# A down projection by seven block products in both halves of the sequence, its weight sums made under the convolution and its gate applied at the end

## The chip, the cores and the metric

The kernel is one decoder layer on one core of a Trainium2 chip. The metric is the device time of one execution in microseconds. Before the change it is 2389.77 us, the median of three runs (2389.1 to 2391.83).

## The reference

Sequence length 2048, model width 1024, eight attention heads of 64, a short gated convolution beside the attention, and a feed-forward part of width 2816. Cut to what the change touches:

```
h2 = rmsnorm(x, norm2_g) * (1 + sc2) + sh2
u = causal_dwconv(h2 @ w_up, ffn_conv_w)        # (2048, 5632), three taps
u_gate, u_val = jnp.split(u, 2, axis=-1)
y = (jax.nn.silu(u_gate) * u_val) @ w_down      # (2048, 2816) @ (2816, 1024)
return x + g2 * y
```

All arrays are float32. The gate g2 belongs to the output column, so it may be multiplied into the columns of w_down or applied to the product.

## The kernel before, in words

The layer runs in stages on one core: the modulation and the first norm, the projections of v, k and q, the short convolution (`for j in range(4)`, `for ch in range(4)`, three products of 24 matmuls each), the attention, the output projection with the second norm, and then up and down, each in two halves of 1024 tokens: `up(0)`, `down_plain`, `up(1)`, `down_seven`.

**Up** goes over 22 pairs of column blocks (128 columns of the gate, 128 of the value). Each pair takes seven block products of 12 float16 matmuls instead of eight, in three PSUM banks X, Y and Z; banks come from ps_d (four banks) for even pairs and from ps_u (three) for odd ones. An eighth bank, ps_n, takes norm2's transposes. In the first half `up_weights` splits the next pair's weights into high and low float16 parts on ScalarE and VectorE, and `keep_weights` stores them; the second half loads them again. After the products come three taps of the convolution (L1495, L1500), silu, and the product y of gate and value (L1513 in the first half, L1517 in the second). `finish` of a pair runs in three steps inside the next pair.

**Down in the first half** (`down_plain`, L1587) stores y to `y_sc` and afterwards goes over four column and row blocks n and 22 steps i. A step loads 512 columns of y and of w_down side by side into one raw tile of 1024 columns (`load_pair`, L1379 to L1385), splits it into a high and a low part (`split_pair`: ScalarE at L1389, VectorE at L1390), and runs four tiles of three matmuls (high by high, high by low, low by high; they are recorded at L146, where `mm3` issues them). Splits run two steps ahead and loads five; the raw tiles and the tiles tagged "hi" and "lo" have four buffers each. The step before a block's last is left out and done together with the last. At the end of a block `add_gated` multiplies each of the four results by the gate and adds x1 (L1204, L1205), then stores it.

Beside this runs a side chain: the last pair's `finish`, then `norm2` for the second half's rows (loads of x1 at L1241, squares on ScalarE at L1245, transposes at L1228, some eleven VectorE operations for each of four column blocks), then the first loads for `up(1)`. One step of it follows steps 0, 1, 2 and then every second one.

**Down in the second half** (`down_seven`, L1623) works with seven products of 11 steps each, 77 for 88. With y and w_down cut into two by two blocks, it needs sums of blocks of y (t1 to t4, made by `down_inputs` in three steps behind each pair of `up(1)` and stored to `y_op`) and of w_down (s1 to s4, made by `down_weights` inside `up(1)` from columns already multiplied by the gate, and stored to `w_op`). The order of the products is in `plan`. The results are collected in two sets of four banks, ps_d for one and ps_u with ps_n for the other; x1 is added in advance on GpSimd (`gadd`, L1640).

**Order.** `K` pins the order of instructions on each engine to that of the program; nearly everything in these stages is pinned, SP's queue of DMA issues too. Stores of the sums are put off: `store_later` notes them and `flush` issues them (L1425) at the start of the next pair, at the start of `down_seven`, and at its fifth step.

Of the kernel before, what the change touches and what calls it, by code (L numbers as in the profile page):

```python
# [46 lines left out]
def kernel(  # L47
# [40 lines left out]
    y_sc = [dram.tile([P, S // 2], F32, name=f"y_sc{i}") for i in range(NPAIR)]  # L88
    y_op = {n: [dram.tile([P, 512], F32, name=f"y_{n}_{j}") for j in range(NJ)] for n in ("b11", "b21", "b22", "t1", "t2", "t3", "t4")}
    w_op = {n: [dram.tile([P, D], F32, name=f"w_{n}_{j}") for j in range(NJ)] for n in ("a11s3", "a12a22", "s1s2", "s4")}  # L90
# [62 lines left out]
    with ExitStack() as ph:  # L153
# [587 lines left out]

        def up_scales():
# [53 lines left out]
        for j in range(4):  # L796
# [5 lines left out]
            for ch in range(4):  # L802
# [7 lines left out]
                for name in ("x", "c", "b"):  # L810
# [379 lines left out]
    with ExitStack() as ph:  # L1190
# [188 lines left out]
        def load_pair(n, i):  # L1379

            Q, hf = divmod(n, 2)
            raw = raw_tile()
            K(nc.sync.dma_start(raw[:, 0:512], y_sc[i][:, Q * 512 : (Q + 1) * 512]))
            K(nc.sync.dma_start(raw[:, 512:1024], w_down[i * P : (i + 1) * P, hf * 512 : (hf + 1) * 512]))
            return raw  # L1385

        def split_pair(raw):
# [6 lines left out]
        plan = (("a11", "b11"), ("s2", "t2"), ("a12", "b21"), ("s3", "t3"), ("s1", "t1"), ("a22", "t4"), ("s4", "b22"))  # L1394
        place = {
            "a11": ("a11s3", 0), "s3": ("a11s3", 1), "a12": ("a12a22", 0), "a22": ("a12a22", 1), "s1": ("s1s2", 0), "s2": ("s1s2", 1),
            "s4": ("s4", 0),
        }

        def load_operands(p, j):  # L1400

            w, y = plan[p]
            n, e = place[w]
            raw = raw_tile()
            K(nc.sync.dma_start(raw[:, 0:512], y_op[y][j]))
            K(nc.sync.dma_start(raw[:, 512:1024], w_op[n][j][:, e * 512 : (e + 1) * 512]))
            return raw
# [3 lines left out]
        def first_pairs(load, hv):  # L1411

            for i in range(3):
                raws[0, i] = load(0, i)
# [16 lines left out]
        def down_inputs(i, y):  # L1431

            j = i // 2
            a, b = y[:, 0:512], y[:, 512:1024]
            if i % 2 == 0:
                t12 = fq.tile([P, 1024], F32, tag="lo", name="t12", bufs=4)
                K(nc.sync.dma_start(y_op["b11"][j], a))
                sub(t12[:, 0:512], b, a)
                store_later(y_op["t1"][j], t12[:, 0:512])
# [4 lines left out]
            K(nc.sync.dma_start(y_op["b21"][j], a))  # L1444
            K(nc.sync.dma_start(y_op["b22"][j], b))
# [3 lines left out]
            store_later(y_op["t2"][j], t12[:, 512:1024])  # L1449
            store_later(y_op["t3"][j], t34[:, 0:512])  # L1450
            store_later(y_op["t4"][j], t34[:, 512:1024])

        def down_weights(j):

            wa, wb = [fp.tile([P, 1024], F32, tag="first", name="wd", bufs=2) for _ in range(2)]
            for e, w in enumerate((wa, wb)):
                K(nc.sync.dma_start(w, w_down[(2 * j + e) * P : (2 * j + e + 1) * P, :]))
            yield
            wc, wd = [fq.tile([P, 1024], F32, tag="lo", name="wd", bufs=4) for _ in range(2)]
            a11, a21, a12, a22 = wa[:, 0:512], wa[:, 512:1024], wb[:, 0:512], wb[:, 512:1024]  # L1460
            s1, s2, s4 = wc[:, 0:512], wc[:, 512:1024], wd[:, 0:512]
            for w in (wa, wb):
                K(V.tensor_tensor(w, w, gates[:, D : 2 * D], op=ALU.mult))
                yield
            add(s1, a21, a22)
            sub(a21, a11, a21)
            yield
            sub(s2, s1, a11)
            sub(s4, a12, s2)
            for n, w in (("a11s3", wa), ("a12a22", wb), ("s1s2", wc)):  # L1470
                store_later(w_op[n][j], w)
            store_later(w_op["s4"][j][:, 0:512], s4)
            while True:
                yield

        def up(hv):
# [25 lines left out]
            def finish(i, p1, Y, gate, val, yg):  # L1502
# [19 lines left out]
            last = wsum = None  # L1522
            for i in range(NPAIR):
# [13 lines left out]
                else:  # L1537
                    wts = first_pairs(load_operands if hv else load_pair, hv)
                ops = next(wts)
                if hv and i % 2:  # L1540
                    next(wsum)
# [17 lines left out]
                if hv == 0:  # L1559
                    keep_weights(i)  # L1560
                elif i % 2:
                    next(wsum)
                else:
                    wsum = down_weights(i // 2)
                    next(wsum)
# [21 lines left out]
        def down_plain(side):  # L1587
# [32 lines left out]
            for _ in side:  # L1620
                pass
# [123 lines left out]
```

## Time and profile before

| what | us |
|---|---|
| median of three runs | 2389.77 |
| lowest, highest | 2389.1, 2391.83 |
| the profiled execution | 2394.71 |
| its span, first to last instruction | 2393.0 |
| TensorE busy | 2304.5 (96%) |
| VectorE busy | 1723.5 (72%) |
| ScalarE busy | 1172.7 (49%) |
| GpSimd busy | 358.6 (15%) |
| HBM traffic over the span | 178 GB/s |

In the profile PE is TensorE's matmul, PEld its weight load, DVE VectorE, ACT ScalarE, POOL GpSimd and SP the engine that issues most DMAs; a q behind the name is the engine's instruction queue. L1390 is line 1390 of the kernel. A row of the groups gives the engine, the operation, what is written and read with its shape, how many there are, their busy time in all and the mean of one in nanoseconds, then the idle time of the engine just before them and what ended most of it. A row of the chain gives start, duration and what the chain passed through. A row of the timeline gives start, duration, engine and line; the bracket at its end is the idle time of the engine before it and what released it. Times are microseconds from the first instruction. The busy time of matmuls that overlap is counted once, so their mean duration is longer than their pace.

### The profile page before, as it was taken

Reading aid. Unit: us, or ns where it says so; the run is one execution under the profiler, and the core shown is the slowest. Engines: PE = TensorE matmul, PEld = TensorE weight load, DVE = VectorE, ACT = ScalarE, POOL = GpSimd, SP = SyncE. Lnnn points to the kernel's source line nnn. Section 1 sums busy time; section 2 is a strip of 40 time slices with the busy share of each in tenths; the row PEclk is TensorE's granted clock in tenths of the full one; section 3 lists DMA queues with packets and bytes.
Section 4 is the critical chain, followed back from the end, with each engine's and each line's share of the span. In section 5 each row is a group of like instructions: output and inputs, shape, how many; then the busy total and the mean of one; then the engine's idle time right before and its main releaser. Section 6 shows DMA issues by size and latency. Waiting matters only on the chain.

```text
span 2393.0 us, 38865 instructions
## 1 busy us (share of the span) xinstructions
PE 2304.5 (96%) x14340; PEld 1385.3 (58%) x14340; DVE 1723.5 (72%) x3345; ACT 1172.7 (49%) x1997; POOL 358.6 (15%) x294
## 2 busy tenths in 40 slices
PE   5899999999899898999999999999999999998999
PEld 5765554444677676444444444688864444446887
DVE  6768885553999887466888888757747777676554
ACT  5745454320788896343655655555522222224332
POOL 0211111011677783001000000000000000000021
PEclk9999999999999999999999999999999999999999
DMA  9446596522899997434555554777666676675765
GB/s 264 148 147 186 158 263 187 155 83 84 164 183 190 196 191 166 137 119 158 181 180 199 193 181 169 261 232 239 219 217 224 212 268 214 217 266 188 245 228 194
DMA packets 447895, 461.03 MB, mean 193 GB/s; under 512 B 190720, under 2 KB 300632, under 8 KB 446680
## 3 DMA queue, kind: packets, MB, share of 16 engines
q1 hardware_dynamic: 440584, 441.70, 61.5%
q10 hardware_dynamic: 4752, 8.46, 1.0%
q0 software_dynamic: 2368, 8.39, 1.0%
q8 instruction: 112, 1.84, 0.3%
q14 instruction: 79, 0.65, 0.1%
HBM read 290.60 MB, written 134.28 MB: 178 GB/s over the span
## 4 chain that ended last, share of the span: by engine, by line
PE 86%; DVE 6%; ACT 3%; DMA 2%; issue 2%; SPq 1%; POOL 0%; DVEq 0%; ACTq 0%; POOLq 0%
PE acc L1487 33%; PE acc L146 22%; PE pr L146 10%; PE acc L1699 8%; PE pv L146 3%; PE pt L1068 2%; PE ps L1007 1%; PE ps L1008 1%; DVE near L1075 1%; PE po L1104 1%; DMA far<-wide 1%; DVE s_t L1031 1%; PE po L1106 1%; PE po L1105 1%; ACT s_t L1048 1%
## 5 line engine op out<-in xcount | busy, mean ns | idle before, releaser
L1487 PEld LDWEIGHTS <-pair 128*128 128x128 f16 x3696 | 361.6, 98 | 436.1 <-issue 0.3
L1487 PE MATMUL acc<-t,pair 128*128 128x512 f16 x2112 | 477.4, 379 | 0.0
L1487 PE MATMUL acc<-b,pair 128*128 128x512 f16 x1584 | 363.4, 379 | 0.0
L1390 DVE TENSOR_TENSOR lo<-raw,hi 128x1024 fp32r<-128x1024 f32 x165 | 201.9, 1244 | 138.2 <-ACT hi L1389 135.6
L1500 DVE SCALAR_TENSOR_TENSOR w<-w,fcw,w 128x1024 f32<-128x1024 f32 x176 | 226.1, 1285 | 54.3 <-ACT w L1495 48.1
L1389 ACT ACTIVATE hi<-raw 128x1024 fp32r<-128x1024 f32 x165 | 170.4, 1054 | 166.4 <-PE acc L1699 96.2
L1495 ACT ACTIVATE w<-w,fcw 128x1024 f32<-128x1024 f32 x88 | 100.7, 1144 | 189.1 <-DVE w L1293 189.1
L146 PEld LDWEIGHTS <-h 128*128 128x128 f16 x1344 | 130.2, 98 | 97.5 <-DVE h L359 5.3
L1640 POOL TENSOR_TENSOR u<-u,xs 128x512 f32<-128x512 f32 x4 | 6.0, 1531 | 1175.2 <-DMA raw<-w_s1s 1175.2
L146 PE MATMUL acc<-wp,mp 128*128 128x512 f16 x768 | 169.4, 379 | 1.1 <-DVE raw L960 1.0
L1048 ACT ACTIVATE s_t<-s_t,nb,cst 128x2048 f32<-128x2048 f32 (+15 forms) x128 | 164.7, 1288 | 4.8
L146 PE MATMUL acc<-hi 128*128 128x512 f32 x352 | 139.6, 397 | 1.6 <-DVE t L1204 1.6
L146 PE MATMUL acc<-lo,hi 128*128 128x512 f32 x352 | 137.3, 390 | 0.5 <-DVE lo L1390 0.5
L1060 POOL TENSOR_TENSOR wide<-s_t,wide 128x1024 f16<-128x1024 f32 x64 | 136.6, 2135 | 5.3
L146 PE MATMUL acc<-hi,lo 128*128 128x512 f32 x352 | 137.2, 390 | 0.0
L1031 DVE CUSTOM_DVE_ANT_0 s_t<-ps,nf,mx 128x512 f32<-128x512 f32 (+1 forms) x192 | 119.5, 643 | 17.7 <-PE ps L1010 9.4
L1699 PE MATMUL acc<-hi 128*128 128x512 f32 x308 | 121.4, 394 | 5.7 <-ACT hi L1389 5.7
L146 PE MATMUL pr<-h,wh 128*128 128x512 f16 x576 | 126.5, 379 | 0.0
L146 PE MATMUL pr<-h,wl 128*128 128x512 f16 x576 | 125.8, 379 | 0.0
L146 PEld LDWEIGHTS <-mp 128*128 128x128 f16 x768 | 74.9, 98 | 87.6 <-issue 1.3
L1699 PE MATMUL acc<-lo,hi 128*128 128x512 f32 x308 | 121.1, 393 | 0.9 <-DVE lo L1390 0.9
L1699 PE MATMUL acc<-hi,lo 128*128 128x512 f32 x308 | 120.8, 392 | 0.0
(361 smaller groups left out, 4552.3 us busy)
## 6 DMA issues: line engine op xcount, KB each, us to landing
up_sc<-pair SPq DMA_DIRECT2D x132, 256.0 KB, 3.0
pair<-up_sc SPq DMA_DIRECT2D x132, 256.0 KB, 4.8
wx<-in_w_up_dram SPq DMA_DIRECT2D x88, 256.0 KB, 3.3
raw<-in_w_up_dram SPq DMA_DIRECT2D x44, 512.0 KB, 3.8
raw<-y_sc SPq DMA_DIRECT2D x88, 256.0 KB, 3.2
raw<-in_w_down_dram SPq DMA_DIRECT2D x88, 256.0 KB, 4.2
wm<-in_w_ada_dram SPq DMA_DIRECT2D x128, 128.0 KB, 3.3
y_sc<-w SPq DMA_DIRECT2D x22, 512.0 KB, 2.7
```

The source lines that it names most:

```text
L146: ins = T.matmul(acc, lhsT=a, rhs=b, start=st, stop=sp)
L1007: K(T.matmul(ps[:, 0:cw], lhsT=qt, rhs=kh[:, c0 : c0 + cw], start=True, stop=False))
L1031: K(V.tensor_tensor_reduce(out=s_t[:, o0 + c0 : o0 + c0 + cw], in0=ps[:, 0:cw], in1=nf[:, c0 : c0 + cw], scale=1.0, scalar=-3.0e38 if g == ...
L1048: K(A.activation(cols, cols, AF.Exp, bias=nb[:, p : p + 1], scale=qk[:, 4:5], accum_out=un["l"][:, p : p + 1]))
L1060: K(G.tensor_tensor(wide[:, 1, :], s_t[:, WB * P : WU], wide[:, 0, :], op=ALU.subtract))
L1068: K(T.transpose(pt[:, b * P : (b + 1) * P], s_t[:, (b0 + b) * P : (b0 + b + 1) * P], ident))
L1389: K(A.activation(hi, raw, AF.Copy))
L1390: K(V.tensor_tensor(lo, raw, hi.bitcast(F32), op=ALU.subtract))
L1487: K(T.matmul(acc, lhsT=a, rhs=b, start=st, stop=sp, skip_group_check=True))
L1495: K(A.activation(y, u[:, 0:1024], AF.Copy, scale=fcw[:, ct : ct + 1]))
L1500: K(V.scalar_tensor_tensor(y, u[:, m : m + 1024], fcw[:, m * 44 + ct : m * 44 + ct + 1], y, op0=ALU.mult, op1=ALU.add))
L1699: K(T.matmul(acc[t], lhsT=a[:, c], rhs=b, start=st, stop=sp, skip_group_check=True))
```

## The change

Both halves of down now run the seven products, by one function `down(hv, side)` in place of `down_plain` and `down_seven`.

- The sums of w_down's blocks no longer carry the gate. A new generator `down_sums` makes them once, in the convolution stage, one step behind each product for the first three values of j: two loads of 512 KB and one store of 1 MB for each of 11 pairs of row blocks, and four additions or subtractions on VectorE. `down_weights`, its multiplications by the gate and its stores inside `up(1)` are gone. Blocks that are no sums are read from w_down itself.
- `down_inputs` runs behind each pair of both halves; y is no longer stored as a whole in the first half.
- The gate is applied by `finish_block` when a block is complete, with VectorE multiplying into a temporary and adding it to x1. GpSimd's additions are gone.
- The products stand in another order, in which a product that adds to the block before it follows it in the same banks; four new banks are taken at products 0, 2, 3 and 5, seven different ones in all, and ps_n is left to norm2.
- The side chain advances after steps 0, 1, 2, after even steps, and after steps with e % 7 == 1.

```diff
+        def down_sums():
...
+            for j in range(NJ):
+                if j + 1 < NJ:
+                    load(j + 1)
+                (a11, a21), (a12, a22) = [[w[:, 0:512], w[:, 512:1024]] for w in todo.pop(0)]
+                t = lp.tile([P, 2 * D], F32, tag="ws", name="ws", bufs=1)
+                s1, s2, s3, s4 = [t[:, n * 512 : (n + 1) * 512] for n in range(4)]
+                V.tensor_tensor(s1, a21, a22, op=ALU.add)
+                yield
+                V.tensor_tensor(s3, a11, a21, op=ALU.subtract)
+                V.tensor_tensor(s2, s1, a11, op=ALU.subtract)
+                yield
+                V.tensor_tensor(s4, a12, s2, op=ALU.subtract)
+                nc.sync.dma_start(w_sc[j], t)
+                yield
...
                     if j < 3:
                         next(convs[j + 1][2])
+                    next(wsums)
...
-        plan = (("a11", "b11"), ("s2", "t2"), ("a12", "b21"), ("s3", "t3"), ("s1", "t1"), ("a22", "t4"), ("s4", "b22"))
+        plan = (("a11", "b11"), ("a12", "b21"), ("s2", "t2"), ("s3", "t3"), ("a22", "t4"), ("s1", "t1"), ("s4", "b22"))
...
-                if hv == 0:
-                    K(V.tensor_tensor(yv, yg, yv, op=ALU.mult))
-                    nc.sync.dma_start(y_sc[i], yv)
-                else:
-                    y = fq.tile([P, 1024], F32, tag="hi", name="y", bufs=4)
-                    K(V.tensor_tensor(y, yg, yv, op=ALU.mult))
-                    down_inputs(i, y)
+                y = fq.tile([P, 1024], F32, tag="hi", name="y", bufs=4)
+                K(V.tensor_tensor(y, yg, yv, op=ALU.mult))
+                down_inputs(i, hv, y)
                 yield
...
+            def finish_block(c, n, t, total):
+                g = temp()
+                K(V.tensor_tensor(g, total, gate[n], op=ALU.mult))
+                add(xs[c, n][t], xs[c, n][t], g)
+                K(nc.sync.dma_start(out[rows[c][t], n * 512 : (n + 1) * 512], xs[c, n][t]))
 
             def evict(p, t):
                 a = acc[t]
                 if p == 0:
                     K(A.activation(u2[t], a, AF.Copy))
                 elif p == 1:
+                    finish_block(0, 0, t, a)
+                elif p == 2:
                     add(u2[t], u2[t], a)
...
                 elif p == 3:
                     add(u3[t], u2[t], a)
...
+                elif p == 5:
                     add(u3[t], u3[t], a)
+                    finish_block(1, 1, t, u3[t])
                 else:
+                    g = temp()
+                    add(g, u2[t], a)
+                    finish_block(*((0, 1) if p == 4 else (1, 0)), t, g)
+
+            extra = {(1, 2): (0, 0), (4, 2): (0, 1), (5, 2): (1, 1), (6, 3): (1, 0)}
...
-                if (p, j) == (0, 4):
+                if (p, j) in ((0, 0), (0, 4)):
                     flush()
...
+                if j == 0 and p in (0, 2, 3, 5):
+                    acc = banks({0: "dddd", 2: "uuud", 3: "dddu", 5: "uudd"}[p])
...
-                if e < 3 or e % 2 == 0:
+                if e < 3 or e % 2 == 0 or e % 7 == 1:
                     next(side, None)
...
-        down_plain(chain(up(0), steps[2], steps[3], kept_first()))
-        down_seven(up(1))
+        down(0, chain(up(0), steps[2], steps[3], kept_first()))
+        down(1, up(1))
```

More of the change, by code (lines that the diff above doesn't have):

```diff
@@ L740, in magnitudes, with load @@
                 seen[0] += 1
+        def down_sums():
+            todo = []
+            def load(j):
+                ab = [lp.tile([P, D], F32, tag="wd", name="wd", bufs=4) for _ in range(2)]
+                for e, w in enumerate(ab):
+                    nc.sync.dma_start(w, w_down[(2 * j + e) * P : (2 * j + e + 1) * P, :])
+                todo.append(ab)
+            load(0)
+            yield
[12 more added lines that the diff above has]
+                nc.sync.dma_start(w_sc[j], t)
+                yield
+            while True:
+                yield
+        wsums = down_sums()
         def up_scales():
@@ L1377, in first_weights @@
                 yield
[L1379 to L1385, printed above, removed]
         def split_pair(raw):
@@ L1429, in flush, with down_inputs @@
                 stores.pop(0)()
-        def down_inputs(i, y):
+        def down_inputs(i, hv, y):
             j = i // 2
+            cols = slice(hv * 512, (hv + 1) * 512)
             a, b = y[:, 0:512], y[:, 512:1024]
@@ L1448, in down_inputs @@
             sub(t34[:, 512:1024], a, t12[:, 512:1024])
[L1449 to L1474, printed above, removed]
+            store_later(y_op["t2"][j][:, cols], t12[:, 512:1024])
+            store_later(y_op["t3"][j][:, cols], t34[:, 0:512])
+            store_later(y_op["t4"][j][:, cols], t34[:, 512:1024])
         def up(hv):
@@ L1537, in up @@
                 else:
-                    wts = first_pairs(load_operands if hv else load_pair, hv)
+                    wts = first_pairs(hv)
                 ops = next(wts)
-                if hv and i % 2:
-                    next(wsum)
                 p1 = temp()
@@ L1623, in down_seven, with down @@
-        def down_seven(side):
+        def down(hv, side):
             todo = [(p, j) for p in range(7) for j in range(NJ)]
             loaded = split = 3
-            rows = [[slice((Q * 4 + t) * P, (Q * 4 + t + 1) * P) for t in range(4)] for Q in (2, 3)]
+            rows = [[slice((Q * 4 + t) * P, (Q * 4 + t + 1) * P) for t in range(4)] for Q in (2 * hv, 2 * hv + 1)]
             u2, u3 = [[fb.tile([P, 512], F32, tag=f"src{4 * n + t}", name="u") for t in range(4)] for n in range(2)]
+            gate = [gates[:, D + n * 512 : D + (n + 1) * 512] for n in range(2)]
@@ L1634, in x1_tiles, with banks @@
                     K(nc.sync.dma_start(xp, x1_sc[r.start // P][:, n * 512 : (n + 1) * 512]))
-            def write(c, n, t, src):
-                K(nc.sync.dma_start(out[rows[c][t], n * 512 : (n + 1) * 512], src))
-            def gadd(o, a, b):
-                K(G.tensor_tensor(o, a, b, op=ALU.add))
+            def banks(kinds):
+                return [
+                    ps_d.tile([P, 512], F32, tag="d", name="acc") if k == "d" else ps_u.tile([P, 512], F32, tag="u", name="acc")
+                    for k in kinds
+                ]
+            def finish_block(c, n, t, total):
[3 more added lines that the diff above has]
+                K(nc.sync.dma_start(out[rows[c][t], n * 512 : (n + 1) * 512], xs[c, n][t]))
             def evict(p, t):
```

109 lines of the change are left out of this document (21 added, 88 removed).

## The prediction

> **What bounds the kernel now.** I read the stretches by stage first, then the chain that ended last, then the waits inside single stages. Five stretches matter: the convolution group stage that gets the new weight sums, the two windows of up in the first half, down in the first half (plain), and down in the second half (seven products). The columns are microseconds, then each engine's busy time and instructions, the granted clock, the DMA share and GB/s.
>
> ```profile
> 340.00:598.00 258.00, 258.00 (x1221) 121.29 (x1220) 132.58 (x289) 71.96 (x161) 35.10 (x38) 1.00 0.45 137
> 1112.00:1316.00 204.00, 204.00 (x947) 92.47 (x946) 171.99 (x194) 114.28 (x169) 2.16 (x4) 1.00 0.49 172
> 1316.00:1519.00 203.00, 203.00 (x942) 92.27 (x941) 177.94 (x197) 118.71 (x176) 0.00 (x0) 1.00 0.54 189
> 1519.00:1771.00 252.00, 249.92 (x1125) 203.79 (x1124) 168.75 (x208) 123.72 (x148) 0.00 (x0) 1.00 0.70 233
> 2169.00:2393.00 224.00, 213.26 (x925) 174.94 (x923) 120.36 (x112) 82.98 (x81) 20.38 (x12) 0.97 0.67 225
> ```
>
> TensorE is the bound in all of them; it is idle only in down. But VectorE is busy for 178 of 203 us in up of the first half, and there the change adds work. The chain (start, length, what) and the groups give the pace of a down matmul and the counts:
>
> ```profile
> 1119.96 398.86 PE acc L1487 x1848
> 1518.82 40.84 PE acc L146 x180
> 1770.26 398.88 PE acc L1487 x1848
> 2169.13 5.48 PE acc L1699 x24
> 2174.63 0.70 DVE wd L1294
> 2175.35 0.75 SPq L1425
> 2177.38 4.44 DMA raw<-w_a11s
> 2183.02 1.24 DVE lo L1390
> 2204.57 184.37 PE acc L1699 x812
> 2389.03 0.69 DVE xs L1293
> L146 PE MATMUL acc<-hi 128*128 128x512 f32 x352 | 139.6, 397 | 1.6 <-DVE t L1204 1.6
> L1699 PE MATMUL acc<-hi 128*128 128x512 f32 x308 | 121.4, 394 | 5.7 <-ACT hi L1389 5.7
> ```
>
> 812 matmuls in 184.37 us is 0.227 us each, so a step (four tiles by three matmuls) takes 2.72 us. Each group is one of three alike: plain has 3 x 352 = 1056 matmuls, seven products have 3 x 308 = 924. Up takes 398.9 us for 22 pairs, 18.1 each. Plain runs from 1518.82 to 1770.26, 251.4 us against 1056 x 0.227 = 239.8; of the other 11.6, 2.1 is visible idle (252.00 less 249.92) and 9.5 goes with norm2's transposes. Seven runs from 2169.13 to 2388.94, 219.8 us against 209.8: all 10.0 lost lies before 2204.57.
>
> **The change, part by part.** The sum is made against the profiled execution, 2394.7 us (span 2393.0), 4.9 above the median of 2389.8; I carry its difference over to the median.
>
> *Matmuls of the first half:* 132 fewer, 132 x 0.227 = -30.0 us, all on the path.
>
> *Start of down in the second half.* What cost the 10.0 us is this row:
>
> ```profile
> 2171.91 0.69 DVE L1293 TENSOR_TENSOR wd<-wd 128x512 f32<-128x512 f32 x1 [5.62 <-PE acc L1699]
> ```
>
> The sums of the last w_down pair need a "lo" buffer; the three first operand pairs and t12 hold all four, so VectorE stands until TensorE has used up the first one. Behind it stand the stores of the sums (SP, L1425), behind those the next loads: the chain above. down_weights is deleted, so -10.0. Its other VectorE work lay beside a full TensorE: nothing.
>
> *Sums of w_down in the convolution stage.* 44 additions of about 0.69 us are 30 us of VectorE, which has 125 us free there. The transfers, 22 of 0.5 MB and 11 of 1 MB, are 23 MB in 34 steps of 5.4 us (258 us for 48 products): 125 GB/s on top of 137 at a share of 0.45, about 0.86 in all. Six PSUM banks, two chunks of three products, cover a VectorE that is late by less than a chunk, 16 us. I take 0; without cover a few late weights, up to 3.
>
> *Up of the first half.* Each pair's y now goes through down_inputs: one subtraction for even pairs, three for odd ones. They are in the second half's trace already; beside them stand the rows of the first half where they will be inserted:
>
> ```profile
> 2141.54 0.69 DVE L1294 TENSOR_TENSOR t<-y,t 128x512 f32<-128x512 f32 x1
> 2142.15 0.68 DVE L1294 TENSOR_TENSOR t<-y 128x512 f32<-128x512 f32 x1
> 2142.75 0.68 DVE L1294 TENSOR_TENSOR t<-y,t 128x512 f32<-128x512 f32 x1
> 1314.32 0.68 DVE L1293 TENSOR_TENSOR t<-t,acc 128x512 f32<-128x512 f32 x1
> 1316.83 0.69 DVE L1293 TENSOR_TENSOR w<-t,acc 128x512 f32<-128x512 f32 x1 [1.04 <-PE acc L1487]
> 1323.68 2.61 DVE L1500 SCALAR_TENSOR_TENSOR w<-w,fcw,w 128x1024 f32<-128x1024 f32 x2 [0.54 <-ACT w L1495]
> ```
>
> They start 0.6 us apart: 0.7 for an even pair, 1.9 for an odd one (0.1 because the first must wait for y), 2.6 for two. VectorE's idle time in two pairs of 18.1 us is 2 x (1.04 + 0.54) = 3.2. So it fits, barely, but not everywhere: in odd pairs u3 (1314.32) is read 1.9 us later, ending at 1316.9 to 1317.0, and Y's last product, which writes that bank next, wants to start when Z's is over, just before 1316.83, at about 1316.65. That is 0.36 us for each of 11 odd pairs: +4.0. Bounds: 0, and 11 x 2.6 = 28.6 if none of the idle time is of use. I take 4.0, as the idle rows are there. SP issues 3.5 small stores a pair for one large one; only prefetches stand behind them.
>
> *Down of the first half, what appears.* Here side work (norm2) runs in the same strict order of queues, in 77 steps for 88. These rows price it:
>
> ```profile
> 1530.35 2.39 SPq L1241 DMA_DIRECT2D w<-x_sc  x4
> 1537.12 1.06 ACT L1245 ACTIVATE junk<-w 128x1024 bf16<-128x1024 f32 x1 [3.57 <-DMA w<-x_sc]
> 2192.97 3.55 SPq L1425 DMA_DIRECT2D y_t<-t  x3
> 1643.03 0.68 DVE L1204 TENSOR_TENSOR t<-acc,gates 128x512 f32<-128x512 f32 x1
> 1643.74 0.69 DVE L1205 TENSOR_TENSOR xs<-xs,t 128x512 f32<-128x512 f32 x1
> 1644.35 0.68 DVE L1204 TENSOR_TENSOR t<-acc,gates 128x512 f32<-128x512 f32 x1
> ```
>
> A. norm2(2) loads x1 at step 4; the squares follow 6.8 us after the issue and ScalarE stands (3.57 us) with every later split behind it. Now the two y stores, a load whose buffer waits for t12's and t34's "lo" buffers, and three t stores go ahead on SP: the issue moves from 11.5 us after down's start to about 17, data come at 24, two squares (2.3), a split on ScalarE (1.05) and the match on VectorE (1.24) end at 28.7. TensorE wants that pair at 9 x 2.72 = 24.5: 4.2, and 0.5 more for the pair after it: 4.7 (0 to 6).
>
> B. norm2(3) loads at step 28 and, by the new e % 7 == 1, squares at step 29, not two steps later. ScalarE's wait grows by 2.72 us, and step 31 is the one that TensorE skips and does together with 32, so it wants two pairs at once and runs out when the data come: 2.3 + 1.05 + 0.6, and 1.05 for the low half: 5.0 (0 to 6).
>
> C. An eviction has now three dependent additions or products where it had two: 0.71 + 0.71 + 0.61 = 2.03 us a tile, 8.1 for four, after the fifth, sixth and seventh products. After the fifth (step 54) norm2(3)'s next ScalarE instruction waits for a subtraction queued behind the 8.1, and the split stands behind that: 8.1 + 0.7 + about 1.8 + 1.05 against two pairs ready (5.44): 6.2, with 0.3 for the low half 6.5 (2.5 to 7.5, the former if VectorE starts evicting 4 us before the product's end).
>
> D. The end of the fourth product, where norm2 works in two steps running: 2.0 (0 to 2.2). At the end of the sixth the seventh adds into the same banks; the fourth tile's first addition ends 2.9 us after the product, TensorE wants the bank at 9 x 0.227 = 2.0: 0.9 at least, with a split ahead of it 1.8, with norm2's rest 4.0 (0.9 to 5).
>
> E. Half clock. In the trace of before, two long waits of TensorE (the row gives the sum, the times and the longest) are each followed by 6.8 us at a clock of 0.50:
>
> ```profile
> PE po L1104 <- DVE at L1112: 4.4, 1, 4.4
> ...
> 926.70:933.50 6.80, 5.28 (x60) 5.09 (x59) 3.41 (x10) 5.07 (x9) 0.69 (x1) 0.50 0.51 108
> ...
> PE acc L1699 <- ACT hi L1389: 5.7, 1, 5.7
> ...
> 2179.40:2186.20 6.80, 2.69 (x6) 1.80 (x7) 3.15 (x3) 3.99 (x4) 0.00 (x0) 0.50 0.97 312
> ```
>
> 6.8 us at half speed cost 3.4 at most, and part of it passes idle (2.69 of 6.80 busy the second time). I count 2.4 once, for C, between 0 and 3.4; A and B have gaps of 3 to 4 us and I leave them at full clock.
>
> The Trainium skill, "TensorE: Matmul & The Clock Gate", section "HAM oscillation — how this bites in real kernels", says that idle gaps over some 3.4 us bring the clock down; by it A and B, which lie at that edge, may pay too. The trace agrees for the waits above, 4.4 and 5.7 us.
>
> First half's down: 209.8 + 9.5 + 4.7 + 5.0 + 6.5 + 2.0 + 4.0 + 2.4 = 243.9 for 251.4: -7.5. So most of the 30.0 is given back to queues.
>
> *Down of the second half:* no side work. -10.0; +0.8 at the fifth product's end (evictions until 4.2 us after it, a split to 5.4, just what is ready; 0 to 2); +1.8 at the sixth's; tail: the last tile ends 4.3 us after the last matmul (four tiles of 2.03, starting 4.08 - 0.2 before it) for 0.8 now (2388.94 to 2389.72), +3.5. Together -3.9.
>
> Sum: -7.5 - 3.9 + 4.0 = -7.4: 2387.3 for the profiled execution, 2382.4 against the median. 0.2% is 4.8 us, about what a measurement of this kernel tells from no change; faster is below 2385.0.
>
> **Rivals.** *The queues catch up.* If A to E and the bank waits are absorbed as today's 3.57 us wait is (no TensorE idle follows it), down of the first half is 209.8 + 9.5 + 2.1 = 221.4 (-30.0), of the second -10.0 + 3.5, up 0: -36.5, 2353. For it: today's plain loses 2.1 us visibly. Against: VectorE has 168.8 of 252 us there and the same work in 30 us less.
>
> *VectorE becomes the bound in up, slower than before.* If its idle time can't be shifted, each two pairs cost 2.6 us: 28.6 for 4.0, +17.2, 2407. It decides once up loses 11.4 us more than before. For it: 3.2 us idle against 2.6. Against: 0.36 us a pair makes room for the next.
>
> *Half clock at A and B too*, 3.4 us each and C's at its full 3.4: +7.8, about 2390, no change. By the page's rule this is possible; a gap of 3 us may or may not do it.
>
> **How the numbers follow.** Forecast 0.57 (own range 2372 to 2391), queues catch up 0.17, half clock everywhere 0.15, VectorE-bound up 0.11. Faster: 0.57 x 0.7 + 0.17 = 0.57; same 0.16 + 0.10 = 0.26; slower 0.17. The range reaches halfway to the first rival and beyond the clock's: 2360 to 2396, with some 0.1 outside on either side.
>
> **What would show it.** Right: down of the first half about 244 us with TensorE idle near its steps 9, 31, 57 and after the sixth product; ScalarE's longest waits there for x1; no idle at the second half's start; up about 403 us for 398.9; VectorE running 4 us past the last matmul. Wrong: a first-half down near 221 us, or up over 410.

## The result, and the profile after

The changed kernel takes 2398.93 us, the median of five runs (2397.5 to 2403.06), against 2389.77 us for five of the kernel before, measured beside it: 1.0042 times the time, 95% interval 1.0027 to 1.0057. It is slower by 9.2 us; the forecast was 7.4 us faster.

The profiled execution of after took 2397.5 us (span 2395.8). These are its stretches from the first half's up on, with the columns of the prediction (us, then each engine's busy time, the clock, the DMA share, GB/s):

```profile
1128.00:1530.00 402.00, 400.07 (x1848) 180.62 (x1847) 373.01 (x429) 231.88 (x345) 0.64 (x2) 1.00 0.57 201
1530.00:1777.00 247.00, 229.35 (x990) 184.05 (x989) 168.03 (x215) 114.38 (x141) 0.00 (x0) 0.96 0.65 217
2176.00:2395.00 219.00, 210.22 (x924) 172.72 (x922) 131.37 (x135) 81.50 (x80) 0.00 (x0) 0.99 0.66 214
```

In the second row TensorE is idle for 17.6 of 247 us and its mean clock is 0.96: the first half's down has 132 matmuls fewer and is only 4.6 us shorter. The chain of work that ended last gives the borders of the stages (start, length, what):

```profile
1127.77 38.86 PE acc L1489 x180
1530.15 10.92 PE acc L1643 x48
1776.96 398.88 PE acc L1489 x1848
2175.83 144.20 PE acc L1643 x636
```

Up of the second half again takes 398.88 us, and the chain passes through the first 636 matmuls of the second half's down without a break: the idle start of before is gone. But the first half's up starts at 1127.77, not at 1119.96. The delay is there well before. Each of these rows is one form of the convolution's matmuls, from its first product on, with the shortest, median and longest duration in nanoseconds, then the start of the first and the last in microseconds; one fence is before, the other after:

```profile
L146 PE MATMUL pr<-h,wh x576: 376/379/390, 341.4 to 534.5; 128*128 128x512 f16 x192
```

```profile
L145 PE MATMUL pr<-h,wh x576: 376/379/390, 347.1 to 540.9; 128*128 128x512 f16 x192
```

So 5.7 us are lost before the convolution begins, in the projections of k and q, where the diff has no line. The additions of `down_sums` are the first suspects. They stand behind the convolution's products in the program, but they are not held by `K`, and were placed much earlier. In after, the rows of the loads and of one of the four additions:

```profile
L748 SPq DMA_DIRECT2D wd<-in_w_down_dram x22: 328/432/1437, 184.1 to 416.5; - x22
L761 DVE TENSOR_TENSOR ws<-wd x11: 680/684/692, 190.3 to 424.0; 128x512 f32<-128x512 f32 x11
```

They begin at 190, 157 us before the stage that was to hide them: 28 of the 44 start in the projections, by 282.2, and the other 16 inside the convolution. A part of the projections and then the whole stretch in before, and the whole stretch in after:

```profile
260.00:300.00 40.00, 40.00 (x201) 20.12 (x200) 35.47 (x123) 24.57 (x53) 4.32 (x7) 1.00 0.75 208
155.00:336.00 181.00, 180.48 (x919) 91.93 (x918) 155.47 (x595) 89.52 (x206) 19.00 (x31) 1.00 0.70 198
```

```profile
155.00:336.00 181.00, 174.94 (x867) 86.84 (x865) 161.24 (x598) 84.75 (x196) 19.51 (x30) 0.99 0.88 264
```

Before, TensorE was full there (180.48 of 181) with VectorE busy for 155.5; after, VectorE has 5.8 us more and TensorE 5.5 less, and from 310.5 to 314.0 TensorE's clock is at half (0.51). TensorE's waits in this stretch, which in before come to one of 0.5 us, come to 6.3 in after, nearly all for ScalarE's step `tf`, which itself waits for VectorE eight times, 6.8 us in all. The two largest groups of TensorE's waits (us in total, times, longest):

```profile
PE pt L623 <- ACT tf L629: 2.5, 2, 2.2
PE pm L691 <- ACT tf L629: 1.7, 1, 1.7
```

In sum, from the two traces: 7.8 later at up(0), of which 5.7 by the convolution's start; up of the first half 402.4 for 398.9 (+3.5); its down 246.8 for 251.4 (-4.6); up of the second half the same; its down, to the span's end, 220.0 for 223.9 (-3.9). That is +2.8, as the spans say. Of the 7.8, 2.1 come between the convolution and up, where the two kernels differ only in a rest of the sums; over all fourteen profiles of this case that stretch takes from 775.5 to 783.1 us, so 2.1 is within its scatter. The medians differ by 6.4 more; on that, below.

### The profile page after: what moved, and what is told of

Read it like the earlier page. It is cut to its first block, busy times and chain, and to the rows that moved or that the text cites. A ratio compares the mean times of both kernels' runs of the same rounds, so it can differ in the third digit from the quotient of the medians.

```text
span 2395.8 us, 38576 instructions
## 1 busy us (share of the span) xinstructions
PE 2284.4 (95%) x14208; PEld 1359.9 (57%) x14208; DVE 1738.1 (73%) x3404; ACT 1161.1 (48%) x1990; POOL 340.0 (14%) x282
## 4 chain that ended last, share of the span: by engine, by line
PE 72%; DVE 14%; DMA 5%; ACT 4%; issue 3%; SPq 1%; POOL 0%; DVEq 0%; ACTq 0%; POOLq 0%
PE acc L1489 28%; PE acc L1643 14%; PE pr L145 10%; PE acc L145 8%; PE pv L145 2%; PE pt L1099 2%; PE ps L1038 1%; PE ps L1039 1%; DVE near L1106 1%; DMA far<-wide 1%; DVE t L1324 1%; PE po L1135 1%; DVE s_t L1062 1%; DVE lo L1413 1%; PE po L1137 1%
## 5 line engine op out<-in xcount | busy, mean ns | idle before, releaser
L1413 DVE TENSOR_TENSOR lo<-raw,hi 128x1024 fp32r<-128x1024 f32 x154 | 185.2, 1223 | 128.4 <-ACT hi L1412 114.6
L1643 PE MATMUL acc<-hi 128*128 128x512 f32 x616 | 245.5, 399 | 15.0 <-ACT hi L1412 10.2
L1643 PE MATMUL acc<-lo,hi 128*128 128x512 f32 x616 | 243.9, 396 | 4.7 <-DVE lo L1413 4.7
L1643 PE MATMUL acc<-hi,lo 128*128 128x512 f32 x616 | 242.9, 394 | 0.0
L1412 ACT ACTIVATE hi<-raw 128x1024 fp32r<-128x1024 f32 x154 | 158.8, 1053 | 165.3 <-PE acc L1643 96.6
L1643 PEld LDWEIGHTS acc<-hi 128*128 128x128 f32 x616 | 117.5, 191 | 43.6 <-ACT hi L1412 12.3
L1643 PEld LDWEIGHTS acc<-lo,hi 128*128 128x128 f32 x616 | 117.4, 191 | 31.4 <-DVE lo L1413 7.7
L1643 PEld LDWEIGHTS acc<-hi,lo 128*128 128x128 f32 x616 | 117.4, 191 | 24.8
L1038 PE MATMUL ps<-kh,qs 128*128 128x512 f16 (+1 forms) x320 | 109.6, 347 | 5.3 <-DVE mx L1062 4.4
```

Source lines behind the costliest of these rows:

```text
L1038: K(T.matmul(ps[:, 0:cw], lhsT=qt, rhs=kh[:, c0 : c0 + cw], start=True, stop=False))
L1412: K(A.activation(hi, raw, AF.Copy))
L1413: K(V.tensor_tensor(lo, raw, hi.bitcast(F32), op=ALU.subtract))
L1643: K(T.matmul(acc[t], lhsT=a[:, c], rhs=b, start=st, stop=sp, skip_group_check=True))
```

## The experiments

**The theories.** Theory 1: the sums of w_down cost VectorE time where it has none to spare. Theory 2: their transfers do. Theory 3: the loss lies in the first half's down. The table gives each run's median, its ratio to the kernel before (with 95% interval; the medians of before beside these runs are 2390.0 to 2391.1, on several chips, so the ratio is the safer comparison), the start of the convolution's first product, and the lengths of the first half's up, its down, and the second half's down (to the span's end) in the profiled execution. Stages are counted from first matmul to first matmul as the chain gives them; the expectations count down from slightly earlier, some 0.3 us more.

| run | us | ratio (interval) | conv. starts | up 1 | down 1 | down 2 |
|---|---|---|---|---|---|---|
| before | 2389.8 | | 341.4 | 398.9 | 251.4 | 223.9 |
| after | 2398.9 | 1.0042 (1.0027-1.0057) | 347.1 | 402.4 | 246.8 | 220.0 |
| e1 | 2390.6 | 1.0003 (0.9995-1.0011) | 338.7 | 402.4 | 247.6 | 220.1 |
| e2 | 2387.7 | 0.9989 (0.9981-0.9998) | 338.3 | 402.4 | 247.9 | 219.8 |
| e3 | 2387.8 | 0.9991 (0.9981-1.0000) | 348.8 | 402.4 | 235.4 | 220.5 |
| e4 | 2398.4 | 1.0036 (1.0024-1.0048) | 337.4 | 410.5 | 247.6 | 220.9 |
| e5 | 2385.5 | 0.9979 (0.9971-0.9988) | 338.3 | 402.4 | 247.3 | 214.2 |
| e6 | 2386.4 | 0.9984 (0.9974-0.9994) | 338.8 | 398.9 | 247.7 | 219.9 |
| e7 | 2374.8 | 0.9935 (0.9923-0.9947) | 339.0 | 398.9 | 242.5 | 214.2 |
| e8 | 2386.8 | 0.9981 (0.9972-0.9990) | 339.3 | 398.9 | 251.7 | 217.9 |
| e9 | 2377.6 | 0.9946 (0.9932-0.9959) | 339.1 | 398.9 | 243.1 | 214.3 |
| e10 | 2400.7 | 1.0047 (1.0035-1.0060) | 350.9 | 402.4 | 248.9 | 219.9 |
| e11 | 2362.4 | 0.9880 (0.9866-0.9895) | 337.4 | 398.9 | 232.7 | 214.3 |
| e12 | 2364.2 | 0.9886 (0.9870-0.9903) | 338.7 | 398.9 | 233.6 | 214.2 |

**e1: the sums held in program order.**

```diff
-                    nc.sync.dma_start(w, w_down[...])
+                    K(nc.sync.dma_start(w, w_down[...]))
...
-                V.tensor_tensor(s1, a21, a22, op=ALU.add)
+                K(V.tensor_tensor(s1, a21, a22, op=ALU.add))
...
-                nc.sync.dma_start(w_sc[j], t)
+                K(nc.sync.dma_start(w_sc[j], t))
```

> The kernel after, with the loads, additions and stores of down_sums kept in program order, so that they stay beside the convolution's products. Theory 1 (the sums were planned into the k and q projections, where VectorE has no time to spare): the convolution's first product starts near 341.5 us as in the kernel before, not at 347.1, the stage ends near 583 for 589, and the time falls by 5 to 8 us, to about 2392. Theory 2 (the 23 MB of transfers delay the stage that they stand in, whichever it is): the projections end at 341.5, but the convolution then loses the 5 to 6 us, and the time stays within 2 us of 2399. Theory 3 (the loss of the medians comes from the first half's down and its half-clock windows): at most 2 us less.

The median is 2390.56, that of the kernel before beside it 2391.09. The convolution's start, the first sums and the projections in e1:

```profile
L145 PE MATMUL pr<-h,wh x576: 376/379/391, 338.7 to 531.8; 128*128 128x512 f16 x192
L759 DVE TENSOR_TENSOR ws<-wd x11: 683/694/1137, 354.0 to 512.8; 128x512 f32<-128x512 f32 x11
155.00:336.00 181.00, 180.48 (x908) 90.71 (x906) 157.86 (x606) 90.76 (x209) 18.99 (x32) 1.00 0.70 199
```

The sums now start at 354 and the projections are full again (180.48). And beside the convolution they cost nothing: from its first to its last start it takes 193.1 us, as in before. This is a part of the convolution in e1, TensorE busy for all of it at a DMA share of 0.84:

```profile
360.00:520.00 160.00, 160.00 (x756) 74.98 (x755) 117.50 (x243) 56.62 (x131) 19.40 (x21) 1.00 0.84 290
```

So the prediction's price for this part, nothing, was right for the place that it assumed, and the place was wrong. Pinning is worth 8.4 us between the two medians, and 8.4 at the convolution's start (347.1 to 338.7). That is slightly more than the 5 to 8 expected, and far from theory 3's 2 at most. With it the time is that of before, not under it.

**e2: the transfers without the additions.** What is left out: the sums; the blocks are stored as they were loaded.

```diff
-                t = lp.tile([P, 2 * D], F32, tag="ws", name="ws", bufs=1)
-                V.tensor_tensor(s1, a21, a22, op=ALU.add)
...
-                nc.sync.dma_start(w_sc[j], t)
+                for e, w in enumerate(ab):
+                    nc.sync.dma_start(w_sc[j][:, e * D : (e + 1) * D], w)
```

> The kernel after with the 44 additions of down_sums left out: the loads of w_down and the stores to w_sc are made, unpinned, of the blocks as they are loaded, so the sums are missing from the result. Theory 1: with VectorE free of them the first product of the convolution starts by 342 us, and the time is 4 to 7 us under the kernel after. Theory 2: the transfers alone delay the projections, the first product starts at 346 to 347 and the time stays within 2 us of the kernel after. Theory 3: no change over 2 us.

The loads are as early as in after, and the projections don't mind:

```profile
L748 SPq DMA_DIRECT2D wd<-in_w_down_dram x22: 327/423/1688, 183.6 to 395.2; - x22
155.00:336.00 181.00, 180.48 (x907) 90.56 (x905) 157.59 (x608) 91.35 (x209) 19.35 (x32) 1.00 0.93 283
```

With a DMA share of 0.93 TensorE is as full as in before. Theory 2 falls, and with e1 the additions on VectorE in the projections are shown to be the cause. (e2 is 11.2 us under after where 4 to 7 were expected, and 2.9 under e1. The two profiles differ by 2.9 us between the convolution and up, where the scatter from profile to profile is larger; why the medians differ stays open.)

**e10: time or waiting?** Does VectorE lose its own 0.69 us per addition, or the wait for the one tile that is still being stored? Seven smaller tiles, still unpinned:

```diff
-                t = lp.tile([P, 2 * D], F32, tag="ws", name="ws", bufs=1)
-                s1, s2, s3, s4 = [t[:, n * 512 : (n + 1) * 512] for n in range(4)]
+                s1, s2, s3, s4 = [lp.tile([P, 512], F32, tag="ws", name="ws", bufs=7) for _ in range(4)]
...
-                nc.sync.dma_start(w_sc[j], t)
+                for n, t in enumerate((s1, s2, s3, s4)):
+                    nc.sync.dma_start(w_sc[j][:, n * 512 : (n + 1) * 512], t)
```

> The kernel after with the sums unpinned as there, but with seven tiles of 512 columns in place of one of 2048 and a store for each sum, so that an addition hardly waits for a store. If the loss in the projections is the wait of VectorE's queue for the store of the pair before: the convolution starts by 343 us and the time falls by 4 to 8 us, to 2391 to 2395. If it is VectorE's time, taken where it has none to spare: the convolution starts at 345 to 349 still, and the time stays within 3 us of 2399.

The time is 2400.7, within the 3 us of the second case, and the convolution starts at 350.9, later still (in its profile TensorE's clock is at half for 10.2 us of the projections, for 3.4 in after). VectorE's waits in this stretch, after first and then e10:

```profile
DVE ws L761 <- DMA wd<-in_w_down_dram: 3.3, 1, 3.3
DVE ws L759 <- DMA w_sc<-ws: 2.7, 4, 0.9
```

```profile
DVE ws L758 <- DMA wd<-in_w_down_dram: 8.0, 4, 3.1
DVE ws L758 <- DMA w_sc<-ws: 0.7, 1, 0.7
```

The wait for the store went from 2.7 to 0.7, and that for the loads from 3.3 to 8.0: an early addition at the head of VectorE's queue waits for one or the other, and the projections' work stands behind it. So the one buffer isn't the cause. How much of the loss is the additions' own time and how much their waits for loads isn't separated.

**e3: norm2's steps moved in the first half's down.** The prediction's A, B and C said that three gaps there come from side work ahead of the splits.

```diff
                     K(nc.sync.dma_start(xn[Q][t], x1_sc[Q * 4 + t]))
                 yield
+                if Q == 2:
+                    for _ in range(3):
+                        yield
...
-                if e < 3 or e % 2 == 0 or e % 7 == 1:
+                if e < 3 or e % 2 == 0 and e % 11 != 10 or e % 11 in (3, 5):
```

> The kernel after with another timetable of norm2 in the first half's down: x1 is loaded at step 3 and its squares come at step 8 instead of 4 and 6, none of its steps falls on the last step of a product, and the second x1 load has four steps before its squares instead of one. The sums stay unpinned. If the idle time near the 9th, 31st and 57th step came from this side work standing ahead of the splits, as the prediction had it: the gaps of 4.9, 3.9 and 7.3 us go, with up to three half-clock windows of 3.4 to 6.8 us that follow them; first half's down 228 to 235 us for 246.8, the time 2380 to 2388. Rival: the splits wait for the raw loads and for buffers that the stores of the y sums hold, whatever the side work does: first half's down stays over 242.

Down takes 235.4 us and the median falls by 11, though the sums are still unpinned (the convolution starts at 348.8). So the first half's down has much to give as well. The prediction's theory of it holds, though down is just above its range: B's idle time (3.1 us in after) is gone, A's falls from 3.7 to 3.2 and C's from 6.2 to 4.2. TensorE's idle time in this stage falls from 17.6 to 11.7 us, and its stretches at half clock from four, 20.5 us in all, to two, 6.8 us. What C was in after can be read from the chain. TensorE's last matmul ahead of the gap starts at 1707.14:

```profile
1699.39 2.35 DVE lo L1413 x2
1701.74 0.61 DVE t L1324
...
1709.24 0.69 DVE xs L1324
1709.93 0.61 DVE t L1252
1710.55 0.02 issue
1710.57 0.77 ACT t L1242 x2
...
1712.24 0.96 ACT hi L1412
1713.20 0.02 issue
1713.22 1.24 DVE lo L1413
1714.46 0.04 issue
1714.50 3.91 PE acc L1643 x11
```

Twelve eviction steps on VectorE from 1701.74 to 1709.93, behind them norm2's subtraction (L1252), behind that ScalarE's conversion, and only then the split that TensorE waits for: the order that the prediction gave for C.

**e4: two subtractions of `down_inputs` on GpSimd** (on top of e1).

```diff
-            sub(t34[:, 0:512], b, b12)
-            sub(t34[:, 512:1024], a, t12[:, 512:1024])
+            sub_g(t34[:, 0:512], b, b12) if hv == 0 else sub(t34[:, 0:512], b, b12)
+            sub_g(t34[:, 512:1024], a, t12[:, 512:1024]) if hv == 0 else sub(t34[:, 512:1024], a, t12[:, 512:1024])
```

> As e1, and in the first half's up two of the three subtractions behind each odd pair (t3 and t4) run on GpSimd, which is idle there (1.70 us for such an addition in the kernel before). If VectorE's lack of time there costs the 3.5 us: up of the first half takes 398.9 to 399.5 us instead of 402.4, and the time is 3 to 3.5 us under e1. Rival: VectorE's operations grow longer beside GpSimd, or the delay comes from the wait for y and not from the count of subtractions: up stays at 401 to 403 or more, and the time within 1.5 us of e1 or above it.

It loses 7.8 us against e1: up takes 410.5, so the rival came true. The rows of one odd pair, GpSimd and then VectorE:

```profile
1315.07 1.72 POOL L1327 TENSOR_TENSOR t<-y 128x512 f32<-128x512 f32 x1 [33.50 <-issue]
1316.76 2.24 POOL L1327 TENSOR_TENSOR t<-y,t 128x512 f32<-128x512 f32 x1
```

```profile
1315.58 2.29 DVE L1245 TENSOR_TENSOR pair<-raw,pair 128x1024 f16<-128x1024 f32 x1
1317.91 1.64 DVE L1325 TENSOR_TENSOR raw<-t,raw 128x512 f32<-128x512 f32 x1
...
1335.16 1.22 DVE L1245 TENSOR_TENSOR pair<-raw,pair 128x1024 f16<-128x1024 f32 x1
1336.42 0.69 DVE L1325 TENSOR_TENSOR raw<-t,raw 128x512 f32<-128x512 f32 x1
```

The last two rows are from the next pair. There, where GpSimd works on nothing, the same two VectorE operations take 1.22 and 0.69 us. Beside GpSimd each is longer by about 1 us and ends 1.1 and 0.6 us, nearly its usual time, after the GpSimd instruction that was running (which ended at 1316.79 and 1319.00). So 1.4 us taken off VectorE came back as 2.0. TensorE's waits for VectorE's additions at L1324 in this stage rise from 1.9 us in e1 to 10.1.

**e6: the same two subtractions, later on VectorE** (on top of e1): after u3 and the value's addition of the next pair.

```diff
-            sub(t34[:, 0:512], b, b12)
-            sub(t34[:, 512:1024], a, t12[:, 512:1024])
...
+            def late():
+                sub(t34[:, 0:512], b, b12)
+                sub(t34[:, 512:1024], a, t12[:, 512:1024])
...
                 add(val[:, 514:1026], u3, p5)
+                if last:
+                    next(last, None)
```

> As e1, and in both halves' up the subtractions for t3 and t4 of an odd pair come after u3 and the value's addition of the next pair, not ahead of them. If the 3.5 us of the first half's up are the wait of the odd pair's last product for u3 behind the three subtractions: up takes 398.7 to 399.5 us for 402.2, the time is 3 us under e1, and down starts by that much earlier. Rival: VectorE has no idle time to give, so the delay only goes to the gate's addition or to the first weights of the next pair: up stays at 401 to 403.

The chain passes through up without a break:

```profile
1118.40 398.86 PE acc L1493 x1848
```

398.86 us is the time of before, with the same additions made. In e1 TensorE's only waits in this stage are ten for an addition at L1324, 1.9 us in all; in e6 it has none. So the 3.5 us came from the order on VectorE: the two subtractions stood ahead of u3 and the value's addition. The edit moves them behind both, so it doesn't tell the two apart. The median is 4.2 under e1.

**e5: shorter evictions** (on top of e1).

```diff
+            def gather(p, t):
+                c, n = blocks[p]
+                g = temp()
+                K(V.tensor_tensor(g, (u3 if p == 5 else u2)[t], gate[n], op=ALU.mult))
+                add(xs[c, n][t], xs[c, n][t], g)
...
+                else:
+                    finish_block(*blocks[p], t, a)
...
+                if p > 3 and 5 <= j <= 8:
+                    gather(p, j - 5)
```

> As e1, and the evictions are shortened: u2 or u3 times the gate is added to x1 four steps before a product's end, one tile a step, so that at the end each tile needs one product with the gate and one addition, 1.3 us on VectorE, no more than the 1.36 us in which TensorE finishes a tile. If the idle time after the fifth and sixth products is VectorE's queue of evictions: the 7.3 us near step 57 and the half clock that follows them go, as does most of what the sixth product's end loses, first half's down takes 234 to 240 us for 247.9 in e1, and the last matmul is followed by 1.5 us instead of 4.3, second half's down 217 to 218 us for 220.4; in all 10 to 16 us under e1. Rival: the 16 more VectorE operations and norm2's, which keep their place, take the time away again: down of the first half stays over 244.

Half came true. The second half's down takes 214.2 us for 220.1, more than expected; its chain has no break until the last product:

```profile
2169.23 205.43 PE acc L1644 x906
```

The first half's down stays at 247.3, as the rival said. ScalarE's longest waits there at the ends of the fifth and sixth products (1690 to 1735) are for VectorE operations of norm2:

```profile
ACT t L1242 <- DVE t L1252: 12.5, 2, 8.8
ACT t L1242 <- DVE t L1317: 9.2, 2, 5.9
```

**e7 and e9: the parts together, with two more timetables.** Both have e1, e5 and e6, and load x1 one tile a step. e7 uses e3's steps and those with e % 11 == 7; e9 has a list of steps.

> Sums pinned (e1), shorter evictions (e5), later subtractions (e6), and a timetable like that of e3 in which x1 comes one tile a step over four steps. If the four are independent: down of the first half 226 to 232 us, up 399, second half's down 217.5, the time 2390 - 18 - 3 - 3 = 2366, from 2360 to 2372. If the loads of w_down and the stores of the sums of y set the first half's down: down stays over 238 and the time over 2374.

> As e7, with norm2's steps in the first half's down given by a list: the cheap ones (transposes of the third group, loads of x1) one to a step until step 25, the dear ones (some 8 us of VectorE for each of four column blocks) two steps apart from step 36 on, none on a product's last step. If the 242.7 us of e7 came from dear steps standing in consecutive steps: down of the first half 228 to 234 us, and the time 2360 to 2367. Rival: the waits move on to other places, 238 to 243, and the time stays within 4 us of 2375.

2374.8 and 2377.6: faster than both kernels, but both miss. Down takes 242.5 and 243.1 us, more than e3's 235.4, so the parts are not independent; whether the timetables or e5's added VectorE operations did that isn't separated. e9's theory, dear steps in a row, fell. In e9 TensorE's longest gap, 4.08 us from one start to the next at 1684.4, follows ScalarE's longest wait for norm2, 5.9 us until 1682.8:

```profile
ACT t L1242 <- DVE t L1319: 19.8, 4, 5.9
```

This conversion comes from norm2: `high(t4)` waits for an addition of its own step, and the splits stand behind it.

**e11 and e12: no conversion waits for its own step.** On top of the parts of e7, with e3's and e9's timetables.

```diff
+                if k:
+                    high(t4, t4s[0])
+                    low(t4, *t4s)
                 b1 = columns(Q, k)
-                if k:
-                    low(t4, *t4s)
...
                 high(b2, t2s[0])
-                yield
                 diff(t4, b21[1], b2)
+                K(V.tensor_tensor(t4, t4, b21[0], op=ALU.add))
                 low(b2, *t2s)
-                K(V.tensor_tensor(t4, t4, b21[0], op=ALU.add))
+                yield
+            if Q % 2:
                 high(t4, t4s[0])
-                yield
-            if Q % 2:
                 low(t4, *t4s)
```

`high(t4)`, `high(b1)` and `high(b2)` now stand at the heads of the steps behind those that make their inputs.

> Sums pinned, shorter evictions and later subtractions as in e7, with e3's timetable of norm2's steps, and with norm2's steps for the odd groups rewritten so that no conversion on ScalarE waits for a VectorE operation of its own step: it comes at the head of the next step. If what is left in e7 and e9 is the splits on ScalarE standing behind such conversions (a wait of 5.94 us for t in e9, just ahead of TensorE's 4.08): down of the first half 226 to 234 us for 242.7, and the time 2360 to 2368. Rival: the loads, or VectorE's own time, set it whatever the order: over 238, and the time within 4 us of 2375.

> The same rewritten steps with the list of e9. If the order on ScalarE was the cause in both timetables: 226 to 234 us for 243.3 in e9, the time 2362 to 2369 for 2377.6. Rival: the timetable matters more than the order: over 238 here and under 236 in e11.

Down falls to 232.7 and 233.6 us, and the times are in both ranges. e9 and e12 differ in this rewriting alone, and there ScalarE's waits for the additions of t4 (L1319) fall from 19.8 us to this:

```profile
ACT t L1242 <- DVE t L1319: 4.9, 2, 3.2
```

So in the list's timetable the order on ScalarE was the cause of some 9.5 us. For e3's timetable there is no run with e5 and without the rewriting, so e11 agrees with this but doesn't show it by itself. With the order right, the two timetables differ by 1.0 us in down. e11's stretch of down:

```profile
1514.00:1747.00 233.00, 224.96 (x991) 181.74 (x990) 177.52 (x232) 115.23 (x141) 0.00 (x0) 0.98 0.69 232
```

TensorE is idle for 8.0 us, for 17.6 in after, with 9.5 us more work on VectorE. At 2362.4 us e11 is faster than both kernels, 0.988 times the time of before (0.9866 to 0.9895).

**e8: what the wait at the second half's start was worth in the kernel before.**

```diff
+            if j < NJ - 1:
+                wc, wd = [fq.tile([P, 1024], F32, tag="lo", name="wd", bufs=4) for _ in range(2)]
+                s1, s2, s4 = wc[:, 0:512], wc[:, 512:1024], wd[:, 0:512]
+            else:
+                s1, s2, s4 = [fb.tile([P, 512], F32, tag=f"src{n}", name="wd") for n in range(3)]
```

> The kernel before with one edit: for the last pair the sums of w_down go to three tiles that nothing else uses there, so that VectorE doesn't wait for a buffer of the splits. If the 10.0 us at the start of the second half's down came from that wait alone: the first matmuls of down run on without idle time, down takes 214 to 216 us for 224, and the time is 8 to 10 us under before. Rival: with that wait gone the stores of the sums, the loads behind them or the splits behind the last pair's steps come last: 0 to 4 us.

By the median it is 3.4 us (2386.76 for 2390.17; ratio 0.9972 to 0.9990), the rival's size; by the profiled executions 6.0 (217.9 for 223.9). The theory that this wait alone cost the 10.0 us (8 to 10 us expected) fell. The largest wait of TensorE left at that place in e8:

```profile
PE acc L1704 <- DVE lo L1390: 2.5, 3, 1.2
```

## Why the prediction was wrong, point by point

*The step that failed: the sums of w_down in the convolution stage, "I take 0; without cover a few late weights, up to 3".* In up and down nearly everything is held by `K`; the sums are not, and the prediction priced them where the program text has them. They began 157 us earlier, and 28 of the 44 additions ran in a stage where VectorE is busy for 35 of 40 us (the row from 260 to 300 in before). That cost 5.7 us at the convolution's start between the traces of before and after; between all profiled runs with the sums unpinned (347.1, 348.8, 350.9) and those with e1's edit (337.4 to 339.1) it is 8 to 13.5 us, and by the medians of after and e1 8.4. It is about half of the miss. The median was put at 2382.4 and is 2398.9, 16.5 us more: the way to up(0) costs 7.8 for 0, the first half's down 2.9 more than said, its up 0.5 less, and the base, below, 6.4. With e1's edit alone the time is still that of before.

*Up of the first half, +4.0:* measured +3.5. The mechanism given, operations of an odd pair standing ahead of u3 on VectorE, agrees with e6.

*Down of the first half, -7.5:* measured -4.6. The order of the waits was right, and most were smaller than said: TensorE is idle for 3.7 us at A (4.7 said), 3.1 at B (5.0), 6.2 at C (6.5, and C's chain is the predicted one), 1.8 at D (2.0) and 2.2 at the end of the sixth product (4.0). With 0.8 elsewhere these are the 17.6 us. One sign of being right did not hold: ScalarE's longest wait in this stage was not for x1 (6.2 us) but for norm2's subtraction in C (10.6). What was mis-sized on the low side is the half clock, 2.4 us for one stretch. There were four, from 1559.9, 1628.1, 1710.1 and 1747.6. Rows of after, the first and third of them and the time just before:

```profile
1554.00:1560.00 6.00, 2.39 (x7) 0.86 (x6) 2.40 (x2) 3.40 (x7) 0.00 (x0) 0.99 1.01 391
1559.90:1563.30 3.40, 3.20 (x8) 2.52 (x9) 1.60 (x3) 3.34 (x5) 0.00 (x0) 0.50 0.54 174
1707.00:1714.00 7.00, 1.29 (x4) 0.39 (x2) 6.17 (x10) 3.43 (x5) 0.00 (x0) 0.72 0.51 171
1710.10:1716.90 6.80, 3.19 (x7) 2.20 (x8) 6.07 (x9) 3.56 (x5) 0.00 (x0) 0.50 0.55 173
```

In such a stretch matmuls start 0.43 us apart, for 0.23 before and after it, so as an estimate half of TensorE's busy time there is lost: 1.6 us in the first and 1.6 in the third; by their rows the second costs 3.0 and the fourth 1.7:

```profile
1628.10:1634.90 6.80, 6.04 (x15) 4.62 (x15) 4.43 (x5) 3.59 (x6) 0.00 (x0) 0.50 0.68 228
1747.60:1751.00 3.40, 3.40 (x10) 2.65 (x9) 3.37 (x5) 1.06 (x1) 0.00 (x0) 0.50 0.64 184
```

Together some 7.9 for 2.4. So the rival "half clock at A and B too" came true in kind: A and B do have such a stretch, together 4.6 of the 6.8 us that it gave them, and so has the end of the sixth product, which it didn't name. A and B did not have the single gaps of 3 to 4 us that the prediction saw; their gaps come in pieces, none with more than 2.3 us idle. The waits and stretches so counted, with the prediction's 209.8 and 9.5, make 244.8 of the 246.8 us; the last 2.0 stay open.

*Down of the second half, -3.9:* measured -3.9 between the two traces, and by its terms: TensorE waits 0.6 us at the fifth product's end (0.8 said) and 1.4 at the sixth's (1.8), and VectorE ends 4.2 us after the last matmul (4.3). How much of it stands in the medians isn't shown. By e8 the wait of VectorE for a buffer, taken alone, was worth 6.0 us by the profiles and only 3.4 by the medians.

*The base.* The prediction said that the profiled execution of before was 4.9 us over its median and carried the difference over. That execution, 2394.71 us, is slower than all 58 of before that ran beside e1 to e8 (2385.88 to 2394.55). So its difference could not be carried over. A part of its excess can be placed: e8, the same program up to the second half's up, starts its convolution at 339.3 us for 341.4 (against it the sums cost 7.8 us there and not 5.7), and the profile of before has 6.8 us at half clock near 70 us where e8's has 3.4. After the start of the second half's down it has 10.2 us at half clock (2179.4 to 2189.6; the prediction's row gives the first 6.8 of them), which may be missing from other executions as well. The traces of before and after differ by 2.8, the medians by 9.2. Of the 6.4 between, 4.9 is before's profile over its median and 1.4 after's under its own; how they spread over the stages is otherwise not shown, since each kernel's profile is one execution.

*The rivals.* "The queues catch up" is out: the first half's down fell by 4.6 us, not by 30.0. VectorE was not the bound in up as a whole, since moving two operations was enough (e6). That rival was the only one on the slower side, and it looked for VectorE's shortage in the wrong stage.

## What to carry to other kernels

Work that a change says it hides under a stage lies there only if something holds it there: look for what fixes its place on each queue, and if nothing does, price it in the fullest stage that it could reach. In a strict order of queues, try first to move operations behind the one that is waited for: here that took a delay of 3.5 us away, where giving them to another engine added 8.1. An operation that waits for another engine's result of the same step belongs at the head of the next. Before a single profile is used as a base, compare its own time with the median.

## What the runs showed of the hardware

GpSimd's subtractions of 128x512 float32 held up two VectorE operations beside them: in e4 1.22 us became 2.29 and 0.69 became 1.64, each ending nearly as if it had begun when the GpSimd instruction ended. The Trainium skill, "SBUF — State Buffer", section "Who interferes with whom", says that the only contention between engines is over a pair of ports that these two share, and that it is an exclusive lock; the trace agrees, with these rows.

In after, the clock fell to half after TensorE had been idle for 3.6 of 6.0 us in several gaps (1554 to 1560), none of them longer than 2.1 us from one matmul's start to the next, and also in the single gap of 5.7 us. The four stretches of the first half's down last 3.4 or 6.8 us, and the one from 1710.1 began inside that gap, which ended at 1713.2. The Trainium skill, "TensorE: Matmul & The Clock Gate", section "HAM oscillation — how this bites in real kernels", names single gaps of over some 3.4 us; the trace shows less to be enough when gaps come close together.
